# Eight offsets modulo 256 bytes for the weights' high and low parts

## The chip, the cores and the metric

The kernel runs on one core of one Trainium2 chip. The metric is device time in microseconds (us) of one execution of the whole program. Two timed runs of the kernel before gave 2563.72 and 2564.82 us, median 2564.27 us.

## The reference

Two layers on one sequence of 256 positions by 2048 channels, all in float32. Layer 0 is a multi-scale retention of 8 heads, layer 1 a causal attention of 16 heads with a relative-position bias (with 256 positions there is one block, so its block selection never picks anything else). After each comes a gated feed-forward net with a causal convolution of width 3. Nearly all the work is in the products with weights:

```
proj = h @ w_in                 # 2048 x 12288   (q, k, v, g of layer 0)
y @ w_out                       # 4096 x 2048
q, k, v = h @ w_qkv             # 2048 x 6144    (layer 1)
o @ w_out                       # 2048 x 2048
u = h @ w_up ;  ... @ w_down    # 2048 x 11264 and 5632 x 2048, in both layers
```

Each of the two mixers and each feed-forward net starts from an RMS norm and adds its output to the residual; a last RMS norm ends it.

## The kernel before, in words

**Products in high and low parts.** TensorE is fed `float32r` operands. To keep float32 accuracy, each operand is kept as two: a high part (the value copied to `float32r`) and a low part (the value less its high part). A product is then three: high by high, high by low, low by high. Activations are split once and kept (`hT`, `yT`, `actT`, `oT`: for each 128 channels 256 columns of high parts and 256 of low ones). Weights are split as they stream in.

**The stream of weights.** All weights pass through one list of units, each 1 MB: 128 partitions by 2048 floats. SP loads a unit into a tile `raw` (line 153, pool `wraw`, four buffers). Each unit is worked off in halves of 1024 floats (or four parts, where seven products take the place of eight). For each half `issue_split` (line 184) takes a tile `wh` and a tile `wl` of 128 x 1024 `float32r`, 4096 bytes a partition, from the pools `whi` and `wlo` (lines 104, 105, 191, 192), four buffers each. ScalarE (ACT) copies `raw` to `wh` (line 222), VectorE (DVE) subtracts `wh` from `raw` into `wl` (line 223). Line 238 and lines 243, 244 form sums of weight blocks inside `raw` for the seven-product form. `parts[i]` then hands views of both tiles to the matmuls of half `i`.

**The order.** `step` (line 252) issues the splits up to three halves ahead (`LOOKAHEAD`), then the matmuls of one half. A tile `wh` or `wl` comes free when the last matmul that reads it has run; with four buffers, the split of half `i` waits for half `i-4`. In the program built from this, the four buffers of each pool are used in a fixed rotation, but for two places (the 17th and 18th and the 633rd and 634th tile), where two neighbours come in the other order.

**Three kinds of panel use them.**

- `panel_b` (line 330) produces transposed results: a 128 x 128 block of `wh` or `wl` is the stationary operand, which a weight load brings into TensorE, and `xT[k]` of `hT` streams past it: 512 columns (high and low) for `wh` (line 345), 256 columns (high) for `wl` (line 348). One step over `c` is two loads and matmuls of each kind. The q and k projections and both up projections go this way.
- `panel_s` (line 358) and `panel_a` (line 304): a 128 x 128 block of the activations is stationary, and 512 columns of `wh` or `wl` stream past it (line 391, and lines 311 to 313). The v and g projections, the output projections and the down projections go this way; lines 523 to 525 (`mm3`) do the small products of retention and attention, line 541 and 1152 transposes against an identity (`ident`, inside the tile `laid`).

**Where the tiles lie.** The pools are laid one behind the other in each partition, each tile rounded up to 32 bytes. In the program before, `hT` starts at byte 18112, the four `raw` tiles at 56256 and every 8192 bytes on, `wh` at 89024, 93120, 97216 and 101312, `wl` at 105408, 109504, 113600 and 117696, and behind `sml` and `scr` the tiles `yT`, `actT` and `oT`. All of these leave 192 when divided by 256, and all the slices that TensorE reads of them begin at a multiple of 512 bytes in their tile. `h` starts at 0 modulo 256, `ident` at 128, `sg` and `e` at 192.

Of the kernel before, what the change touches and what calls it, by code (L numbers as in the profile page):

```python
# [11 lines left out]
F32R = mybir.dt.float32r  # L12
# [5 lines left out]
P = 128  # L18
# [80 lines left out]
def build(tc, a, out):  # L99
    nc = tc.nc  # L100
    ctx = ExitStack()
    cst = ctx.enter_context(tc.tile_pool(name="cst", bufs=1))
    wraw = ctx.enter_context(tc.tile_pool(name="wraw", bufs=4))
    whi = ctx.enter_context(tc.tile_pool(name="whi", bufs=4))
    wlo = ctx.enter_context(tc.tile_pool(name="wlo", bufs=4))
    sml = ctx.enter_context(tc.tile_pool(name="sml", bufs=2))
    scr = ctx.enter_context(tc.tile_pool(name="scr", bufs=1))
    pacc = ctx.enter_context(tc.tile_pool(name="pacc", bufs=2, space=bass.MemoryType.PSUM))
# [42 lines left out]
    def issue_dma(u):  # L151
        src, n = units[u]
        raws[u] = wraw.tile([P, 2048], F32, name="raw")
        dst = raws[u].rearrange("p (c n) -> p c n", n=n)
        if len(src.shape) == 4:
            for b in range(2):
                nc.sync.dma_start(dst[:, :, b * 512 : (b + 1) * 512], src[:, :, b, :])
        elif u == 2:

            load_x(8, 12)  # L160
            nc.sync.dma_start(dst[:, :4], src[:, :4])
            load_x(12, 16)
            nc.sync.dma_start(dst[:, 4:], src[:, 4:])
        else:
            nc.sync.dma_start(dst, src)
        if u in consts:
            consts[u]()

    def first_dmas():
        (src0, n), (src1, _) = units[:2]  # L170
        for u in range(2):
            raws[u] = wraw.tile([P, 2048], F32, name="raw")
        dst0, dst1 = (raws[u].rearrange("p (c n) -> p c n", n=n) for u in range(2))
        load_x(0, 2)
        nc.sync.dma_start(dst0[:, :2], src0[:, :2])
        load_x(2, 4)
        nc.sync.dma_start(dst0[:, 2:4], src0[:, 2:4])
        nc.sync.dma_start(dst1[:, :4], src1[:, :4])
        load_x(4, 8)
        nc.sync.dma_start(dst0[:, 4:], src0[:, 4:])  # L180
        nc.sync.dma_start(dst1[:, 4:], src1[:, 4:])
        state["dma"] = 2

    def issue_split(i):
        u, split_part = order[i]
        if i == 0:
            first_dmas()
        while state["dma"] <= min(u + (1 if i < 8 else 2), len(units) - 1):
            issue_dma(state["dma"])
            state["dma"] += 1  # L190
        wh = whi.tile([P, 1024], F32R, name="wh")
        wl = wlo.tile([P, 1024], F32R, name="wl")
        if i == 0:
            r = raws[u]

            def split(sl):
                split_to(wh[:, sl], wl[:, sl], r[:, sl])

            def rest():
                x_T(2, 2)  # L200
                split(slice(512, 1024))
                for _ in range(2):
                    issue_split(state["split"])
                    state["split"] += 1

            hi, lo = x_T_parts(0, 2)
            hi(0)
            act.activation(wh[:, :S], r[:, :S], AF.Copy)
            lo(0)
            hi(1)  # L210
            dve.tensor_tensor(wl[:, :S], r[:, :S], wh[:, :S].bitcast(F32), op=ALU.subtract)
            lo(1)
            split(slice(S, 512))
            fillers(FILLERS)
            midway[0, 1] = rest
        else:
            split_part(raws[u], wh, wl)
        n = min(units[u][1], 512)
        parts[i] = (wh.rearrange("p (c n) -> p c n", n=n), wl.rearrange("p (c n) -> p c n", n=n))

    def split_to(hi, lo, src):
        in_turn(act.activation(hi, src, AF.Copy))  # L222
        in_turn(dve.tensor_tensor(lo, src, hi.bitcast(F32), op=ALU.subtract))  # L223
# [28 lines left out]
    def step(n):  # L252
        i = state["mm"]
        ahead = 0 if i == 0 else 1 if i < 3 else 2 if i < 8 else LOOKAHEAD
        while state["split"] <= min(i + ahead, n - 1):
            issue_split(state["split"])
            state["split"] += 1
        halves[i]()
        state["mm"] += 1
# [302 lines left out]
    def x_T(c0, n, how=to_T):  # L562
        return how(hT, c0, lambda t, c: h[:, t, (c0 + c) * P : (c0 + c + 1) * P], c0, n)

    def x_T_parts(c0, n):
        return x_T(c0, n, to_T_parts)
# [115 lines left out]
    def fillers(n):  # L682
        for _ in range(n):
            pe.matmul(warmup[:, :P], lhsT=ones, rhs=ones, start=True, stop=True)
# [556 lines left out]
```

## Time and profile before

| what | value |
|---|---|
| timed runs | 2563.72, 2564.82 us |
| profiled execution, first to last instruction (its span) | 2563.1 us |
| instructions | 34486 |
| granted TensorE clock, mean | 0.999 |

The profiled execution has no time of its own beside the span; the timed runs lie 0.6 and 1.7 us above it.

By stage (busy us of each engine in the stretch):

| stretch, us | stage | PE | PEld | DVE | ACT |
|---|---|---|---|---|---|
| 0 to 75 | start, q and k of head 0 | 72.05 | 59.88 | 61.53 | 47.41 |
| 75 to 515 | retention heads | 439.91 | 372.93 | 386.48 | 236.53 |
| 515 to 741 | last head, output projection | 226.00 | 187.45 | 201.97 | 129.97 |
| 741 to 1234 | up projection, layer 0 | 493.00 | 429.47 | 377.84 | 277.98 |
| 1234 to 1508 | down projection, v of attention | 273.51 | 225.70 | 251.98 | 165.56 |
| 1508 to 1735 | attention | 227.00 | 199.02 | 159.51 | 118.95 |
| 1735 to 1845 | output projection | 110.00 | 91.70 | 90.96 | 64.30 |
| 1845 to 2337 | up projection, layer 1 | 492.00 | 428.89 | 377.22 | 278.40 |
| 2337 to 2563 | down projection, end | 217.55 | 179.30 | 200.58 | 128.43 |

How to read it: PE are the matmuls, PEld the weight loads, which run beside them. Both are pipelined, so the busy time of a matmul (its ns in a row) is longer than the distance from one matmul's start to the next one's; that distance, the pace, is read from start times or from a run of matmuls in the chain of waits. L345 is line 345 of the kernel.

### The profile page before, as it was taken

The numbers are of one execution on the slowest core, as the hardware profiler recorded it, in microseconds if no ns is written. First come the engines' busy times: TensorE is split into PE (matmuls) and PEld (weight loads), VectorE is DVE, ScalarE is ACT, GpSimd is POOL, SyncE is SP. The second block draws the span as 40 slices with busy tenths as digits, with TensorE's granted clock in tenths as the row PEclk, the third lists the DMA queues.
The fourth block names the chain that finished last, engine by engine and source line by source line (L and its number), as shares of the span: only waits on it lengthen the run. The fifth ranks groups of instructions, "written<-read, shape, count | busy, mean of one in ns | idle before, by whom it ended". The sixth has DMA issues, their size and how long they took to land.

```text
span 2563.1 us, 34486 instructions
## 1 busy us (share of the span) xinstructions
PE 2551.0 (100%) x13277; PEld 2174.4 (85%) x13277; DVE 2108.1 (82%) x2766; ACT 1447.5 (56%) x1870; POOL 10.2 (0%) x24
## 2 busy tenths in 40 slices
PE   9999999999999999999999999999999999999998
PEld 7888888888888888888888888888888888888887
DVE  7888888998877777777898887768877777778997
ACT  6555555555555555555565655555655555555654
POOL 0000000000000000000000000000000000000000
PEclk9999999999999999999999999999999999999999
DMA  7665555555565555556665565555556556557654
GB/s 258 229 202 181 197 192 186 182 183 195 197 197 190 197 194 197 194 197 193 234 210 194 198 214 177 175 180 175 194 190 197 194 193 198 192 198 240 215 198 148
DMA packets 342196, 504.41 MB, mean 197 GB/s; under 512 B 9600, under 2 KB 260496, under 8 KB 341776
## 3 DMA queue, kind: packets, MB, share of 16 engines
q1 hardware_dynamic: 330672, 483.53, 56.4%
q10 hardware_dynamic: 11360, 18.69, 2.2%
q8 instruction: 104, 1.70, 0.3%
q14 instruction: 60, 0.49, 0.1%
HBM read 494.82 MB, written 10.51 MB: 197 GB/s over the span
## 4 chain that ended last, share of the span: by engine, by line
PE 95%; DVE 2%; issue 1%; ACT 1%; DMA 1%; SPq 0%; POOL 0%; POOLq 0%; ACTq 0%; DVEq 0%
PE acc L345 34%; PE aux L391 32%; PE acc L348 17%; PE acc L391 8%; DVE wl L223 1%; PE acc L311 1%; PE acc L313 1%; PE acc L312 1%; PE aux L524 0%; PE aux L525 0%; PE aux L523 0%; PE aux L541 0%; DMA raw<-in_ret_w_in_dram 0%; ACT wh L222 0%; DMA f<-t 0%
## 5 line engine op out<-in xcount | busy, mean ns | idle before, releaser
L222 ACT ACTIVATE wh<-raw 128x1024 fp32r<-128x1024 f32 (+2 forms) x1067 | 1084.5, 1028 | 1012.5 <-PE acc L345 439.3
L223 DVE TENSOR_TENSOR wl<-raw,wh 128x1024 fp32r<-128x1024 f32 (+2 forms) x1067 | 1242.0, 1181 | 394.6 <-ACT wh L222 386.6
L345 PE MATMUL acc<-hT,wh 128*128 128x512 f32 x3840 | 1208.8, 396 | 1.0 <-DVE hT L547 0.8
L348 PEld LDWEIGHTS acc<-hT,wl 128*128 128x128 f32 x3840 | 721.0, 188 | 170.4 <-DVE wl L223 0.8
L348 PE MATMUL acc<-hT,wl 128*128 128x256 f32 x3840 | 755.3, 278 | 0.2 <-DVE wl L223 0.2
L345 PEld LDWEIGHTS acc<-hT,wh 128*128 128x128 f32 x3840 | 586.1, 189 | 3.4 <-ACT wh L222 1.6
L391 PE MATMUL aux<-wh,actT 128*128 128x512 f32 x976 | 319.4, 390 | 0.0
L391 PE MATMUL aux<-wh,hT 128*128 128x512 f32 x942 | 314.6, 391 | 0.3 <-ACT wh L222 0.2
L391 PEld LDWEIGHTS aux<-wh,actT 128*128 128x128 f32 x976 | 183.2, 188 | 38.4 <-DVE h L621 0.5
L391 PEld LDWEIGHTS aux<-wh,hT 128*128 128x128 f32 x942 | 176.8, 188 | 38.7 <-ACT wh L222 1.7
L391 PE MATMUL aux<-wl,actT 128*128 128x512 f32 x488 | 189.9, 389 | 0.0
L391 PE MATMUL aux<-wl,hT 128*128 128x512 f32 x471 | 183.8, 390 | 0.4 <-DVE wl L223 0.4
L930 DVE SCALAR_TENSOR_TENSOR t<-u,cw,t 128x256 f32<-128x256 f32 x352 | 146.6, 478 | 0.0
L391 PE MATMUL aux<-wh,yT 128*128 128x512 f32 x426 | 141.8, 391 | 0.4 <-ACT yT L222 0.4
L391 PE MATMUL acc<-wh,hT 128*128 128x512 f32 x358 | 131.6, 391 | 0.0
L391 PEld LDWEIGHTS aux<-wl,actT 128*128 128x128 f32 x488 | 91.6, 188 | 18.8
L391 PEld LDWEIGHTS aux<-wl,hT 128*128 128x128 f32 x471 | 88.4, 188 | 19.1 <-DVE wl L223 1.1
L926 ACT ACTIVATE t<-u,cw 128x256 f32<-128x256 f32 x176 | 94.9, 586 | 0.1
L391 PEld LDWEIGHTS aux<-wh,yT 128*128 128x128 f32 x426 | 80.0, 188 | 17.6 <-ACT yT L222 0.9
L238 DVE TENSOR_TENSOR raw<-raw 128x1024 f32<-128x1024 f32 x77 | 93.6, 1216 | 0.0
L391 PE MATMUL aux<-wl,yT 128*128 128x512 f32 x213 | 83.0, 390 | 0.0
L746 DVE TENSOR_TENSOR bs<-acc,bs 128x512 f32<-128x512 f32 x120 | 81.9, 683 | 0.0
(228 smaller groups left out, 1940.4 us busy)
## 6 DMA issues: line engine op xcount, KB each, us to landing
raw<-in_ffn_w_up_dram SPq DMA_DIRECT2D x176, 1024.0 KB, 5.1
raw<-in_ffn_w_down_dram SPq DMA_DIRECT2D x88, 1024.0 KB, 5.5
raw<-in_ret_w_in_dram SPq DMA_DIRECT2D x133, 512.0 KB, 4.5
raw<-in_moba_w_qkv_dram SPq DMA_DIRECT2D x48, 1024.0 KB, 5.3
raw<-in_ret_w_out_dram SPq DMA_DIRECT2D x32, 1024.0 KB, 5.4
raw<-in_ret_w_in_dram SPq DMA_DIRECT2D x29, 1024.0 KB, 5.5
raw<-in_moba_w_out_dram SPq DMA_DIRECT2D x16, 1024.0 KB, 5.3
f<-t ACTq DMA_DIRECT2D x20, 256.0 KB, 4.2
```

The lines of the kernel that those rows point to most:

```text
L222: in_turn(act.activation(hi, src, AF.Copy))
L223: in_turn(dve.tensor_tensor(lo, src, hi.bitcast(F32), op=ALU.subtract))
L238: dve.tensor_tensor(b[:, 0:2, :], b[:, 0:4:3, :], b[:, 1:2, :].to_broadcast([P, 2, 512]), op=ALU.add)
L311: pe.matmul(acc, lhsT=xh, rhs=wh[:, c, :], start=(k == 0), stop=False)
L312: pe.matmul(acc, lhsT=xh, rhs=wl[:, c, :], start=False, stop=False)
L313: pe.matmul(acc, lhsT=xl, rhs=wh[:, c, :], start=False, stop=(k == nk - 1))
L345: pe.matmul(acc[:, b, :], lhsT=wh[:, c, b * P : (b + 1) * P], rhs=xt[:, k, :], start=(k == 0), stop=False)
L348: pe.matmul(acc[:, b, S:], lhsT=wl[:, c, b * P : (b + 1) * P], rhs=xt[:, k, :S], start=False, stop=(k == KC - 1))
L391: pe.matmul(acc[b], lhsT=xs, rhs=ws, start=(n == 1), stop=(n == uses[b]))
L746: dve.tensor_tensor(bs, acc[:, :, :S], bs, op=ALU.add)
L926: act.activation(t[:, i, :], u[:, i, 2:], AF.Identity, bias=c[:, 3, b : b + 1], scale=c[:, 2, b : b + 1])
L930: dve.scalar_tensor_tensor(t[:, i, :], u[:, i, tap : tap + S], c[:, tap, b : b + 1], t[:, i, :], op0=ALU.mult, op1=ALU.add)
```

## The change

The two pools get one buffer for each of eight tags (`wh0` to `wh3`, `wl0` to `wl3`) in place of four buffers under one name. A tile is 1032 floats long, 4128 bytes, in place of 4096, and half `i` takes the tag `i % 4`. Of the 1032 floats it uses 1024, from the first one on, or for `wh2` and `wl3` from the fifth on (16 bytes further). Nothing else is edited.

```
-    whi = ctx.enter_context(tc.tile_pool(name="whi", bufs=4))
-    wlo = ctx.enter_context(tc.tile_pool(name="wlo", bufs=4))
+    whi = ctx.enter_context(tc.tile_pool(name="whi", bufs=1))
+    wlo = ctx.enter_context(tc.tile_pool(name="wlo", bufs=1))
...
+    def part_tile(pool, name, i, starts):
+        n = i % 4
+        return pool.tile([P, 1032], F32R, name=name, tag=f"{name}{n}")[:, starts[n] : starts[n] + 1024]
+
     def issue_split(i):
...
-        wh = whi.tile([P, 1024], F32R, name="wh")
-        wl = wlo.tile([P, 1024], F32R, name="wl")
+        wh = part_tile(whi, "wh", i, (0, 0, 4, 0))
+        wl = part_tile(wlo, "wl", i, (0, 0, 0, 4))
```

4128 is 16 x 256 + 32, so each tile in the row starts 32 bytes further round the 256 than the one before. With the tiles laid in the order in which they are first taken, the parts used begin at 192, 224, 16 and 32 modulo 256 (`wh0` to `wh3`) and at 64, 96, 128 and 176 (`wl0` to `wl3`). Five of the eight (224, 16, 32, 96, 176) are no multiple of 64; all are multiples of 16. The eight tiles together are 256 bytes longer, so all that lies behind them moves by 256 bytes and keeps its offset modulo 256.

## Prediction

> **What bounds the kernel now.** I read the page first, then the chain of waits, then PE's own waits, then a stretch of the timeline.
>
> ```profile
> span 2563.1 us, 34486 instructions
> ...
> PE 2551.0 (100%) x13277; PEld 2174.4 (85%) x13277; DVE 2108.1 (82%) x2766; ACT 1447.5 (56%) x1870; POOL 10.2 (0%) x24
> ...
> PE 95%; DVE 2%; issue 1%; ACT 1%; DMA 1%; SPq 0%; POOL 0%; POOLq 0%; ACTq 0%; DVEq 0%
> ```
>
> PE is busy all through and holds 95% of the chain that ends last. So the time is the number of matmuls by their pace, and a change of addresses can matter in two ways only: it changes PE's pace, or it makes PE wait. PE's waits for the split tiles are (weight loads, the longest of them; engine, line, what was waited for: us in total, times, longest):
>
> ```profile
> PEld aux L391 <- ACT wh L222: 1.7, 4, 0.6
> PEld acc L345 <- ACT wh L222: 1.6, 2, 1.0
> ...
> PEld aux L391 <- DVE wl L223: 1.1, 2, 0.8
> ...
> PEld acc L391 <- DVE wl L223: 0.9, 1, 0.9
> PEld acc L348 <- DVE wl L223: 0.8, 2, 0.6
> ```
>
> Together 6.1 us in 2563: the splits arrive in time. What is left is the pace. For panel_s it stands in the chain of waits (start us, us, what):
>
> ```profile
> 74.65 5.44 PE aux L391 x24
> ...
> 123.51 5.44 PE aux L391 x24
> ...
> 604.27 5.44 PE aux L391 x24
> ...
> 1254.84 5.44 PE aux L391 x24
> ```
>
> 24 matmuls of 512 columns take 5.44 us, 226.7 ns each, in layer 0's first head, in the output projection and in the down projection alike, with hT, yT or actT as the stationary operand. For panel_b I take the timeline (start us, us, engine and line; L345 x2 opens each step over c):
>
> ```profile
> 999.74 0.62 PE L345 MATMUL acc<-hT,wh 128*128 128x512 f32 x2
> ...
> 1000.44 0.63 PE L345 MATMUL acc<-hT,wh 128*128 128x512 f32 x2
> 1000.46 1.06 ACT L222 ACTIVATE wh<-raw 128x1024 fp32r<-128x1024 f32 x1 [1.74 <-PE acc L345]
> ...
> 1001.13 0.63 PE L345 MATMUL acc<-hT,wh 128*128 128x512 f32 x2
> ...
> 1001.43 0.58 ACT L745 ACTIVATE bs<-acc 128x512 f32<-128x512 f32 x1
> 1001.56 1.23 DVE L223 TENSOR_TENSOR wl<-raw,wh 128x1024 fp32r<-128x1024 f32 x1 [1.57 <-ACT wh L222]
> ...
> 1001.83 0.63 PE L345 MATMUL acc<-hT,wh 128*128 128x512 f32 x2
> ...
> 1002.53 0.63 PE L345 MATMUL acc<-hT,wh 128*128 128x512 f32 x2
> ...
> 1010.89 0.63 PE L345 MATMUL acc<-hT,wh 128*128 128x512 f32 x2
> ```
>
> From 999.74 to 1010.89 are 16 steps: 696.9 ns each, for two matmuls of 512 and two of 256 columns. The reader should see what does not change the step. From 999.74 to 1000.44 DVE is idle from 999.99 on and ACT throughout: 0.70. From 1000.44 to 1001.13 ACT writes a wh tile and DVE is idle: 0.69. From 1001.83 to 1002.53 DVE reads raw and wh and writes wl, with ACT at work too at first: 0.70. If these engines' accesses met PE's in the memory, at one offset modulo 256 or at any, steps with them would be longer. They aren't. Accesses of ACT and DVE cost PE nothing that these 10 ns show.
>
> **The change part by part.** It adds and removes no instruction: the same 1067 splits, 13277 matmuls and loads and DMAs. What can move is the duration of those that touch wh or wl, and the order in which the tiles come free.
>
> ```profile
> L345 PE MATMUL acc<-hT,wh 128*128 128x512 f32 x3840 | 1208.8, 396 | 1.0 <-DVE hT L547 0.8
> L223 DVE TENSOR_TENSOR wl<-raw,wh 128x1024 fp32r<-128x1024 f32 x988 | 1193.2, 1222 | 394.6 <-ACT wh L222 386.6
> L222 ACT ACTIVATE wh<-raw 128x1024 fp32r<-128x1024 f32 x988 | 1035.6, 1059 | 980.2 <-PE acc L345 439.3 <-PE aux L391 193.4 <-issue 155.2
> L348 PE MATMUL acc<-hT,wl 128*128 128x256 f32 x3840 | 755.3, 278 | 0.2 <-DVE wl L223 0.2
> ...
> L391 PE MATMUL aux<-wh,actT 128*128 128x512 f32 x976 | 319.4, 390 | 0.0
> ...
> L746 DVE TENSOR_TENSOR bs<-acc,bs 128x512 f32<-128x512 f32 x120 | 81.9, 683 | 0.0
> ...
> L921 DVE TENSOR_TENSOR u<-bs,rBs 128x512 f32<-128x512 f32 x88 | 60.9, 692 | 3.1
> ...
> L223 DVE TENSOR_TENSOR wl<-raw,wh 128x512 fp32r<-128x512 f32 x78 | 53.2, 683 | 0.0
> ...
> L621 DVE TENSOR_TENSOR h<-h,rBs 128x512 f32<-128x512 f32 x16 | 10.9, 683 | 0.1
> ```
>
> *DVE and ACT.* L223 on 512 columns has both inputs at 192 modulo 256 and takes 683 ns; L621 has h at 0 and rBs at 192 and takes 683 too. Inputs at one offset or at two: no difference, so I take 0. The other bound is L921, which writes u eight bytes past a 32-byte boundary (and reads one input repeated): 692 against 683 of L746, 1.3%. On all of L223 that is 1.3% of 1246 us, 16 us of DVE, in either direction. It is covered by DVE's idle time. The tightest stage is that of the retention heads; first all engines, then L223 alone (stretch: length, busy us):
>
> ```profile
> 75.00:515.00 440.00, 439.91 (x2211) 372.93 (x2210) 386.48 (x505) 236.53 (x285) 5.06 (x8) 1.00 0.59 195
> ```
>
> ```profile
> 75.00:515.00 440.00, 218.99 (x192) 1.00 0.59 195
> ```
>
> DVE has 440.00 - 386.48 = 53.5 us free there, so L223's 219.0 us could grow by 24% before DVE fills the stage. Without that cover the price would be the 16 us, 2580. ACT at 56% has more room. Term: 0.
>
> *PE's pace.* Each matmul reads wh or wl, as the stream (panel_s) or through its weight load (panel_b); its other operand stays at 192. The trace has no PE operand at 16 or 32 modulo 64, but it has one pair of the same work at two offsets, the transposes of L541, where the streamed identity is at 128 and the stationary operand is h at 0 or sg at 192 (ns min/median/max):
>
> ```profile
> L541 PEld LDWEIGHTS acc<-laid,h x64: 138/139/145, 717.5 to 1829.0; 128*128 128x128 f32 x64
> L541 PE MATMUL acc<-laid,h x64: 270/272/331, 717.7 to 1829.1; 128*128 128x128 f32 x64
> L541 PEld LDWEIGHTS aux<-laid,sg x56: 138/141/143, 95.8 to 506.4; 128*128 128x128 f32 x56
> L541 PE MATMUL aux<-laid,sg x56: 272/273/273, 95.9 to 506.5; 128*128 128x128 f32 x56
> ```
>
> 272 against 273, 139 against 141: the load and the matmul take no notice of where the stationary operand lies relative to the stream, 128 apart or 64. I take 0.
>
> The bounds. For a gain, the most that a meeting of PE's own two reads could cost now is the part of the pace that isn't columns. Two equations: 512 s + f = 226.7 and 1536 s + 4 f = 696.9, s ns a column and f ns a matmul with its load. Four times the first less the second gives 512 s = 209.9, so f = 16.8 ns; times 13277 that is 223 us. The nearest row that could be such a meeting is smaller: L345's 396 ns against L391's 390 for the same 512 columns, 6 ns x 3840 = 23 us. For a loss, DVE's 1.3% put on the five tiles of eight that leave the 64-byte raster: 2551 x 5/8 x 1.3% = 21 us. f rests on one fixed cost in both panels, which the trace can't prove; a cost at each switch of weights would explain it without any address, and accesses of ACT and DVE at any phase left PE's step even, so I stay near the small bounds.
>
> The Trainium skill, "TensorE: Matmul & The Clock Gate", part 1, gives back-to-back matmuls of 512 columns 215.7 ns start to start; against the row's 226.7 that leaves 11.0 ns for what comes with each weight load, an estimated 146 us for all, and 2418 if the new offsets removed it. The same page, part 2 (step 1, LDWEIGHTS), states that stationary and streamed operand have independent read ports and that a load takes no bandwidth from the running matmul; by that the 11 ns are no conflict and the change is worth 0. The even step of the trace agrees with the second.
>
> *The order of the tiles.* Before, a split takes whichever tile comes free; after, tile i % 4. In the program before the two are the same but at the two places named above. There a split may wait for the half before it, 16 matmuls at 174 ns (696.9 / 4) = 2.8 us, and splits run three halves ahead, which hides it: 0, at most 2 x 2.8 = 5.6 us. Behind such a wait on ACT stands the next split, and behind that PE. A gain is bounded by the 6.1 us of PE's waits above.
>
> Sum: 2563.1 + 0 = 2563.1 for a profiled span; the runs shown have a median of 2564.27, 1.2 above it, and I carry that: 2564.3 us.
>
> **The rivals.**
>
> *A, faster: PE's two reads meet.* Before, stationary and streamed operand both start at 192; after, seven tiles of eight start elsewhere. For it: f is unexplained, and equal offsets are the rule everywhere in the matmuls. Against it: L541's two rows, and that ACT's and DVE's accesses, which pass PE's at every distance, cost it nothing. Price: 23 us by the nearest row, 2541; all of f would give 2341. It passes 2% (51 us) when 3.9 ns a matmul go.
>
> *B, slower: a start off the 64-byte raster costs PE a piece more.* Place: the five tiles at 224, 16, 32, 96 and 176, in 13277 x 5/8 = 8298 matmuls. For it: L921 shows a small price of an odd start on DVE, and no PE row shows such a start to be free. Against it: only the start of an operand of 512 or 2048 bytes would pay. Price: 21 us by DVE's 1.3%, 2585; with the 6 ns between L345 and L391 on each of the 8298, 50 us, 2614. It decides for slower by over 2% from 6.2 ns on. By the Trainium skill, "SBUF — State Buffer", section on the DMA port swizzle, SBUF is read in lines of 16 bytes; all eight starts are multiples of 16, so by that rule B costs nothing. No row here shows it.
>
> *C: the fixed tags make splits wait*, up to 5.6 us, 2570. PE's short waits speak against it.
>
> *D: the tiles don't move*, if each were rounded up to 256 bytes. Tiles of 8 bytes lie 32 apart before, so no. It would give 2564.3 as well and counts with the forecast.
>
> **How the numbers follow.** Forecast (with D) 0.79, its own range 2558 to 2570 (6 us of waits either way); A 0.11, of which 0.07 over 2%; B 0.07, of which 0.04 over 2%; C 0.03. 2% is about what a measurement of this kernel can tell from no change. So faster 0.07, slower 0.04, the same 0.89. The range goes to the small bounds of A and B, 2541 to 2585; left out are about 0.09 of A and 0.05 of B.
>
> **What would show it.** Right: 24 matmuls of L391 still 5.44 us, a step of panel_b still 696.9 ns, L345 at 396 and L348 at 278, L223 within 1.3% of 1222. A would show as a step under 690 ns or L391 under 225 ns; B as L391's 24 longer than 5.50 us, for some tiles and not for others; C as PEld waits for wh or wl beyond 6 us. The prediction is wrong if PE's pace moves by 2 ns a matmul or more (27 us).

## The result: 28.5 us slower, in the pace of the matmuls

The changed kernel takes 2592.78 us (median of 2592.6 and 2592.97) against 2564.27, a ratio of 1.011 with an interval of 1.0081 to 1.0139. The forecast was 2564.3 and the range ended at 2585.

The page of the profile after, its span, busy times and chain by engine:

```profile
span 2590.8 us, 34479 instructions
...
PE 2579.6 (100%) x13277; PEld 2181.4 (84%) x13277; DVE 2110.7 (81%) x2766; ACT 1450.2 (56%) x1870; POOL 10.2 (0%) x24
...
PE 98%; DVE 1%; issue 0%; DMA 0%; ACT 0%; SPq 0%; POOLq 0%; POOL 0%; ACTq 0%
```

As many matmuls and loads as before, and PE holds still more of the chain. So it isn't waiting longer. The weight loads' waits for the splits, after (the edit moves the lines by four: L391 is now L395, L345 is L349, L348 is L352, L222 is L226, L223 is L227):

```profile
PEld acc L349 <- ACT wh L226: 1.6, 2, 1.0
PEld aux L395 <- DVE wl L227: 1.5, 5, 0.7
PEld aux L395 <- ACT wh L226: 1.3, 5, 0.3
```

4.4 us, where it was 6.1. The groups by shape show that the splits run as they did, and where the time went:

```profile
L349 PE MATMUL acc<-hT,wh 128*128 128x512 f32 x3840 | 1204.4, 395 | 1.4 <-DVE hT L551 1.2 <-ACT wh L226 0.2
L227 DVE TENSOR_TENSOR wl<-raw,wh 128x1024 fp32r<-128x1024 f32 x988 | 1194.3, 1222 | 420.6 <-ACT wh L226 418.9
L226 ACT ACTIVATE wh<-raw 128x1024 fp32r<-128x1024 f32 x988 | 1037.4, 1060 | 1002.9 <-PE acc L349 438.2 <-PE aux L395 228.0 <-issue 161.6
L352 PE MATMUL acc<-hT,wl 128*128 128x256 f32 x3840 | 764.3, 280 | 0.0
...
L395 PE MATMUL aux<-wh,actT 128*128 128x512 f32 x976 | 324.2, 394 | 0.0
```

DVE's subtraction takes 1222 ns as before and ACT's copy 1060 for 1059. The matmul of L395 went from 390 to 394, that of L352 from 278 to 280. These are modelled ends; the pace is read from starts. From the chain of waits (start us, us, what), in the retention heads and in the output projection:

```profile
124.46 5.58 PE aux L395 x24
...
193.63 5.59 PE aux L395 x24
...
602.69 5.59 PE aux L395 x24
...
634.04 5.58 PE aux L395 x24
```

24 matmuls of 512 columns took 5.44 us and now take 5.58. And 16 steps of panel_b on the timeline:

```profile
1013.04 0.62 PE L349 MATMUL acc<-hT,wh 128*128 128x512 f32 x2
...
1024.22 0.62 PE L349 MATMUL acc<-hT,wh 128*128 128x512 f32 x2
```

11.18 us, where it was 11.15.

To see this tile by tile, I matched the matmuls of the trace, in order, with those of the program, which carry the addresses. A "triple" is the three matmuls of panel_s on one stationary pair (high by high, high by low, low by high), a "step" the four matmuls of panel_b; those over 760 ns, or with something else between, are left out. Before, 1520 triples take 681.3 ns on average (680 in the median) and 1824 steps 696.9.

| half (bytes of wh, wl beyond the other operands) | triple after, ns | step after, ns |
|---|---|---|
| 0, 128 | 696.9 | 699.8 |
| 32, 160 | 696.6 | 703.5 |
| 80, 192 | 693.3 | 698.9 |
| 96, 240 | 701.7 | 693.7 |
| mean over all | 697.0 | 699.0 |

(697.0 - 681.3) / 3 = 5.2 ns a matmul, times 4953 matmuls in panel_s and panel_a, would be 25.9 us; (699.0 - 696.9) ns times 1920 steps 4.0 us. That is 29.9 where the span grew by 27.7: the means leave out what lies between panels and the waits. Added up from start to start over every matmul, panel_s and panel_a went from 1131.8 to 1155.3 us, panel_b from 1343.1 to 1347.4, all others from 78.7 to 78.6: 23.5 and 4.3 us, the whole of it. So the loss is in the pace, most of it where the weights are streamed. There every half has its part in it, between 693.3 and 701.7 ns; of the steps, those of the half at 96 and 240 became shorter, 693.7 ns.

### The profile page after: what moved, and what is told of

It is laid out like the page before. It is cut to its first block, busy times and chain, and to the rows that moved or that the text cites. A ratio compares the mean times of both kernels' runs of the same rounds, so it can differ in the third digit from the quotient of the medians.

```text
span 2590.8 us, 34479 instructions
## 1 busy us (share of the span) xinstructions
PE 2579.6 (100%) x13277; PEld 2181.4 (84%) x13277; DVE 2110.7 (81%) x2766; ACT 1450.2 (56%) x1870; POOL 10.2 (0%) x24
## 4 chain that ended last, share of the span: by engine, by line
PE 98%; DVE 1%; issue 0%; DMA 0%; ACT 0%; SPq 0%; POOLq 0%; POOL 0%; ACTq 0%
PE acc L349 34%; PE aux L395 34%; PE acc L352 17%; PE acc L395 8%; PE acc L316 1%; PE acc L315 1%; PE acc L317 1%; PE aux L545 0%; PE aux L528 0%; PE aux L529 0%; PE aux L527 0%; PE acc L545 0%; DMA raw<-in_ret_w_in_dram 0%; DVE wl L227 0%; PE aux L1156 0%
## 5 line engine op out<-in xcount | busy, mean ns | idle before, releaser
L226 ACT ACTIVATE wh<-raw 128x1024 fp32r<-128x1024 f32 (+2 forms) x1067 | 1086.8, 1028 | 1040.9 <-PE acc L349 438.2
L227 DVE TENSOR_TENSOR wl<-raw,wh 128x1024 fp32r<-128x1024 f32 (+2 forms) x1067 | 1243.4, 1182 | 420.6 <-ACT wh L226 418.9
L349 PE MATMUL acc<-hT,wh 128*128 128x512 f32 x3840 | 1204.4, 395 | 1.4 <-DVE hT L551 1.2
L352 PEld LDWEIGHTS acc<-hT,wl 128*128 128x128 f32 x3840 | 720.7, 188 | 166.8
L352 PE MATMUL acc<-hT,wl 128*128 128x256 f32 x3840 | 764.3, 280 | 0.0
L349 PEld LDWEIGHTS acc<-hT,wh 128*128 128x128 f32 x3840 | 589.3, 188 | 4.0 <-ACT wh L226 1.6
L395 PE MATMUL aux<-wh,actT 128*128 128x512 f32 x976 | 324.2, 394 | 0.0
L395 PE MATMUL aux<-wh,hT 128*128 128x512 f32 x942 | 318.3, 395 | 0.0
L395 PEld LDWEIGHTS aux<-wh,actT 128*128 128x128 f32 x976 | 183.1, 188 | 43.8
L395 PEld LDWEIGHTS aux<-wh,hT 128*128 128x128 f32 x942 | 176.7, 188 | 43.0 <-ACT wh L226 1.3
L395 PE MATMUL aux<-wl,actT 128*128 128x512 f32 x488 | 192.2, 394 | 0.0
L395 PE MATMUL aux<-wl,hT 128*128 128x512 f32 x471 | 185.5, 395 | 0.3 <-DVE wl L227 0.3
L395 PE MATMUL aux<-wh,yT 128*128 128x512 f32 x426 | 143.9, 395 | 0.3 <-ACT yT L226 0.3
L395 PE MATMUL acc<-wh,hT 128*128 128x512 f32 x358 | 133.1, 395 | 0.0
L395 PEld LDWEIGHTS aux<-wl,actT 128*128 128x128 f32 x488 | 91.7, 188 | 21.3
L395 PEld LDWEIGHTS aux<-wl,hT 128*128 128x128 f32 x471 | 88.5, 188 | 21.6 <-DVE wl L227 1.5
L395 PEld LDWEIGHTS aux<-wh,yT 128*128 128x128 f32 x426 | 79.9, 188 | 19.8 <-ACT yT L226 0.7
L395 PE MATMUL aux<-wl,yT 128*128 128x512 f32 x213 | 84.0, 395 | 0.0
```

The costliest lines, as they stand in the source:

```text
L349: pe.matmul(acc[:, b, :], lhsT=wh[:, c, b * P : (b + 1) * P], rhs=xt[:, k, :], start=(k == 0), stop=False)
L352: pe.matmul(acc[:, b, S:], lhsT=wl[:, c, b * P : (b + 1) * P], rhs=xt[:, k, :S], start=False, stop=(k == KC - 1))
L395: pe.matmul(acc[b], lhsT=xs, rhs=ws, start=(n == 1), stop=(n == uses[b]))
```

## The experiments

In each kernel the edit moves the line numbers by a few; the tiles' names tell the groups apart. Five theories. DISTANCE: what counts is how far the streamed operand starts from the stationary one, modulo 256, whichever tiles they are. RASTER: a start off a multiple of 64 costs, wherever the other operand lies (rival B of the prediction). ALTERNATION: PE pays when the next streamed operand starts elsewhere than the last. ORDER: the fixed tags make splits wait (rival C). ENGINES: what counts is how wh and wl lie to raw, in the reads and writes of ACT and DVE.

### e1_tags: the tags without the offsets

```
-        wh = whi.tile([P, 1024], F32R, name="wh")
-        wl = wlo.tile([P, 1024], F32R, name="wl")
+        wh = whi.tile([P, 1024], F32R, name="wh", tag=f"wh{i % 4}")
+        wl = wlo.tile([P, 1024], F32R, name="wl", tag=f"wl{i % 4}")
```

(and `bufs=1` in both pools.)

> Only the fixed tags of the change, tiles 4096 bytes long, all eight back at 192 modulo 256. Theory ORDER (the fixed rotation makes splits wait): about 2592 us. Every theory in which the offsets do it: 2564 us within 3, 24 matmuls of a streamed panel in 5.44 us, 16 steps of panel_b in 11.15 us.

Measured: 2564.27 us, ratio 0.9997 (0.9987 to 1.0006). The chain of waits:

```profile
123.79 5.44 PE aux L391 x24
...
133.99 5.44 PE aux L391 x24
```

ORDER falls: all of the loss comes with the offsets.

### e4_all_32: every operand moved together

```
-    sums = cst.tile([P, 48], F32, name="sums")
+    sums = cst.tile([P, 56], F32, name="sums")
```

> All operands from hT on, wh, wl and the activations, moved by 32 bytes together to 224 modulo 256: equal among themselves, but off the raster of 64. DISTANCE and ALTERNATION: 2564 us within 3, triples of 680 ns. RASTER: 2590 us or more, triples of 695 or more.

Measured: 2564.7 us, ratio 0.9999 (0.9989 to 1.0008); triples 681.3, steps 696.9 ns. The chain:

```profile
133.70 5.44 PE aux L391 x24
...
143.90 5.44 PE aux L391 x24
```

RASTER falls: all that PE reads of hT, wh, wl and the activations behind them now starts at 224 modulo 256, off a multiple of 64, and nothing is lost. At this one step of 32 no absolute place matters.

### e2_pairs_a and e3_pairs_b: wh and wl of a half at one offset

One pool in place of two, the tiles in the order wh0, wl0, wh1, wl1 and so on, with lengths and starts that put each pair at its place; for e2:

```
+    def part_tile(name, i, sizes):
+        length, start = sizes[i % 4]
+        return wsp.tile([P, length], F32R, name=name, tag=f"{name}{i % 4}")[:, start : start + 1024]
...
+        wh = part_tile("wh", i, ((1032, 8), (1024, 0), (1024, 0), (1024, 0)))
+        wl = part_tile("wl", i, ((1032, 0), (1032, 0), (1032, 0), (1056, 0)))
```

> wh and wl of one half share an offset; the four halves lie 32, 64, 96 and 128 bytes beyond the other operands (hT, yT, actT, oT, which stay at 192 modulo 256). A triple of the streamed panels (high by high, high by low, low by high) took 680 ns before and 692 to 702 after the change. Theory DISTANCE (what counts is how far the streamed operand starts from the stationary one, modulo 256): every half off 680, 690 to 702, time 2580 to 2600 us. Theory RASTER (a start off a multiple of 64 costs): the halves at 64 and 128 beyond stay at 680, those at 32 and 96 at 695 or more, time about 2578. Theory ALTERNATION (cost when the next streamed operand starts elsewhere than the last): all at 680, 2564 to 2567 us.

> As e2_pairs_a with the four halves 0, 160, 192 and 224 bytes beyond. DISTANCE: the half at 0 has 680 ns a triple, the others 690 to 702, time 2578 to 2595 us. RASTER: 0 and 192 at 680, 160 and 224 at 695 or more, about 2578. ALTERNATION: all at 680, 2564 to 2567 us.

Measured: e2 2600.41 us, ratio 1.0138 (1.0121 to 1.0155); e3 2590.97, ratio 1.0101 (1.0086 to 1.0116). By half:

| bytes beyond the other operands | triple, ns | step, ns |
|---|---|---|
| e2: 32 | 699.8 | 701.7 |
| e2: 64 | 690.3 | 697.3 |
| e2: 96 | 704.2 | 705.8 |
| e2: 128 | 700.3 | 703.4 |
| e3: 0 | 688.6 | 699.6 |
| e3: 160 | 700.7 | 707.6 |
| e3: 192 | 699.4 | 691.9 |
| e3: 224 | 697.8 | 695.4 |

ALTERNATION falls: within a half, wh and wl start at one offset, and no half is at 680. RASTER falls again: it gave 680 ns to the halves at 64, 128 and 192, and they have 690.3, 700.3 and 699.4. DISTANCE passes, but not clean: e2's time and its half at 96 lie just past their ranges (2600 us, 702 ns), and it gave the half at 0 680 ns, and that has 688.6. The trace shows more of this last one. In e3, wl's matmuls on the timeline (one in three), first in a half at 0, then, from 604.81 on, in one at 160:

```profile
602.06 0.40 PE L394 MATMUL aux<-wl,yT 128*128 128x512 f32 x1
...
602.76 0.39 PE L394 MATMUL aux<-wl,yT 128*128 128x512 f32 x1
...
603.45 0.39 PE L394 MATMUL aux<-wl,yT 128*128 128x512 f32 x1
...
604.12 0.39 PE L394 MATMUL aux<-wl,yT 128*128 128x512 f32 x1
...
604.81 0.39 PE L394 MATMUL aux<-wl,yT 128*128 128x512 f32 x1
...
605.51 0.40 PE L394 MATMUL aux<-wl,yT 128*128 128x512 f32 x1
...
606.21 0.40 PE L394 MATMUL aux<-wl,yT 128*128 128x512 f32 x1
```

Within the half at 0 the distances shorten, 0.70, 0.69, 0.67; in the half at 160 they stay at 0.70. Over all halves at 0, the first triple takes 695.9 ns, the second 687.4, the third 681.7 and the fourth 680.5; at 160 it is 698.1, 703.8, 700.4 and 702.4. So a half at distance 0 finds its pace again only after the first two triples, six matmuls, when one at another distance went before. The change has no half with both tiles at 0: the first has wh at 0 and wl at 128.

### e5_raw_96: the source of the splits moved

```
-    rBs = cst.tile([P, 2 * S], F32, name="rBs")
+    rBs = cst.tile([P, 2 * S + 24], F32, name="rBs")[:, : 2 * S]
```

and a tile of 160 bytes behind raw, so that wh and all after it stay at 192 modulo 256.

> Only raw, the source of the splits, moved by 96 bytes; all that TensorE reads stays at 192 modulo 256. Theory DISTANCE (the streamed operand's start against the stationary one's): 2564 us within 3, triples of the streamed panels at 680 ns, steps of panel_b at 697. Theory ENGINES (what counts is how wh and wl lie to raw, through the reads and writes of ACT and DVE): 2580 to 2600 us, triples 690 or more.

Measured: 2564.64 us, ratio 1.0 (0.999 to 1.0009); triples 680 ns in the median, steps 696.9.

```profile
123.62 5.45 PE aux L393 x24
...
133.84 5.44 PE aux L393 x24
```

ENGINES falls at the one distance tried: each tile now starts 160 bytes beyond raw, modulo 256, as wl1 does in the change. (e6 to e9 below add the other side: there the pace changes with raw, wh and wl where they were.) This kernel also puts wh and wl 256 bytes further from hT, and the pace is the same; a move by 256 does nothing, where one by 64 or 128 does.

### e6 to e9: hT moved instead

Here the weights stay where they were. hT gets 64 floats more and begins at another float in each of its four lives (retention, first feed-forward net, attention, second feed-forward net):

```
+    hT_room = cst.tile([P, KC * 2 * S + 64], F32R, name="hT")
+    hT_starts = [4, 8, 12, 16]
+
+    def next_hT():
+        n = hT_starts.pop(0)
+        xT_h[:] = [hT_room[:, n : n + KC * 2 * S].rearrange("p (k s) -> p k s", s=2 * S)]
...
+            if i == 0:
+                after(4, next_hT)
```

> Only hT moved, within a longer tile, by another amount in each of its four lives: 16 bytes in retention, 32 in the feed-forward net of layer 0, 48 in attention, 64 in that of layer 1. wh, wl, raw, yT, actT and oT stay at 192 modulo 256. DISTANCE: panels with yT, actT or oT as stationary operand keep 226.7 ns a matmul; those with hT leave it (229 to 235 ns), and steps of panel_b differ from life to life, between 688 and 708 ns, steady within a life. ENGINES: all panels as before, 2564 us.

> As e6_hT_16_64 with 80, 96, 112 and 128 bytes. DISTANCE: panels with hT off 226.7 ns a matmul and off 697 ns a step, the others as before. ENGINES: all as before, 2564 us.

> As e6_hT_16_64 with 144, 160, 176 and 192 bytes. DISTANCE: panels with hT off 226.7 ns a matmul and off 697 ns a step (where the weights lay 192 bytes beyond hT, in e3_pairs_b, a step took about 690, so some distance in this scan may be faster for panel_b), the others as before. ENGINES: all as before, 2564 us.

> hT moved by 8 bytes in retention, 56 in the feed-forward net of layer 0, 4 in attention, 72 in that of layer 1; the transformed activations of the output and down projections stay at distance 0. DISTANCE with a smooth curve: steps of panel_b near those of the neighbours measured, 690 to 697 ns at 56 and 72 (64 took 690), 697 at 8 and 4. DISTANCE by lines of 16 bytes: 56 as 48 or 64 (702 or 690), 72 as 64 or 80 (690 or 704), 4 and 8 as 0 (697). Panels with actT, yT, oT: 680 ns a triple.

Single runs: 2564.72, 2586.6, 2575.67 and 2587.57 us, each a mixture of four distances. What counts is the pace by distance (mean ns; the feed-forward nets give 697 steps to a distance, the other lives some 210; triples are those with hT as the stationary operand, some 400 in retention, 30 to 72 in the other lives; the row at 0 is the kernel before):

| hT beyond the weights, bytes | step | triple |
|---|---|---|
| 0 | 696.9 | 681.3 |
| 4 | 717.8 | 698.0 |
| 8 | 708.0 | 693.5 |
| 16 | 696.8 | 684.0 |
| 32 | 693.4 | 695.6 |
| 48 | 702.2 | 699.7 |
| 56 | 700.0 | |
| 64 | 690.1 | 699.9 |
| 72 | 708.0 | |
| 80 | 703.6 | 696.3 |
| 96 | 706.7 | 696.0 |
| 112 | 699.5 | 699.9 |
| 128 | 696.7 | 701.9 |
| 144 | 698.9 | 688.3 |
| 160 | 703.3 | 698.8 |
| 176 | 706.1 | 690.8 |
| 192 | 693.4 | 687.3 |

The rows at 4, 48, 112 and 176 are those of attention, where a step takes 699.6 ns in the kernel before too (696.1 to 696.7 in the other lives). Against that, 112 costs nothing.

On the timeline this is 16 steps in the first feed-forward net, of e6 (32 bytes) and then of e7 (96 bytes):

```profile
989.66 0.62 PE L353 MATMUL acc<-hT,wh 128*128 128x512 f32 x2
...
1000.75 0.62 PE L353 MATMUL acc<-hT,wh 128*128 128x512 f32 x2
```

```profile
989.98 0.63 PE L353 MATMUL acc<-hT,wh 128*128 128x512 f32 x2
...
1001.29 0.63 PE L353 MATMUL acc<-hT,wh 128*128 128x512 f32 x2
```

11.09 and 11.31 us, for the same matmuls on weights that lie as they did before. Triples whose stationary operand is yT or actT stay at a median of 680 in e6, e8 and e9 (689.5 for yT in e7, where they take turns with triples on sums of activation blocks, which are kept in hT). The two scans can also be laid side by side: weights x bytes beyond hT are hT 256 - x bytes beyond the weights.

| weights beyond (e2, e3) | step | triple | hT beyond (e6 to e8) | step | triple |
|---|---|---|---|---|---|
| 64 | 697.3 | 690.3 | 192 | 693.4 | 687.3 |
| 96 | 705.8 | 704.2 | 160 | 703.3 | 698.8 |
| 128 | 703.4 | 700.3 | 128 | 696.7 | 701.9 |
| 160 | 707.6 | 700.7 | 96 | 706.7 | 696.0 |
| 192 | 691.9 | 699.4 | 64 | 690.1 | 699.9 |
| 224 | 695.4 | 697.8 | 32 | 693.4 | 695.6 |

The steps come in the same order both times, but for one tie; the triples differ by up to 5.4 ns, and the same distance has the shortest. So the pace follows the distance between the two operands of PE, whichever of them is moved: DISTANCE stands. Not all that was expected under its name came: at 16 and 128 bytes the steps (696.8 and 696.7) did not leave 697, and at 16 and 144 most triples stayed at 680. Of the expectations for e9, both finer forms fail: 8 bytes took 708.0 and 4 took 717.8, neither as 0 nor between 0 and 16, and 72 took 708.0, neither as 64 nor as 80.

The chain of e6 shows that a distance can have two paces. Retention at 16 bytes:

```profile
123.77 5.60 PE aux L399 x24
...
134.16 5.44 PE aux L399 x24
...
144.36 5.44 PE aux L399 x24
```

5.60 at 124, close to the change's 5.58, and 5.44 from 134 on. Triple by triple, hT at 16 bytes runs at 680 ns up to 47 us, at some 700 from 51 to 129, and at 680 from 131 on. At 144 bytes (e8), too, two thirds of the triples take 680 and most of the others some 700. So the triple means of these two rows are of two paces, not of one.

### e11_no_16: the change without the two starts 16 bytes in

```
-        wh = part_tile(whi, "wh", i, (0, 0, 4, 0))
-        wl = part_tile(wlo, "wl", i, (0, 0, 0, 4))
+        wh = part_tile(whi, "wh", i, (0, 0, 0, 0))
+        wl = part_tile(wlo, "wl", i, (0, 0, 0, 0))
```

> The change without its two starts 16 bytes into the tile: wh at 0, 32, 64, 96 and wl at 128, 160, 192, 224 beyond the other operands. If the loss of the change came from those two odd starts (theory LINE16): 2564 to 2570 us. DISTANCE: six of the eight distances are as they were and the other two are off 0 as well: 2580 to 2600 us, triples of the half at wh 0, wl 128 at about 697 ns as in the change.

Measured: 2590.29 us, ratio 1.01 (1.0084 to 1.0115), the change's loss but for 2.5 us. The half at 0 and 128, the same in both kernels, has triples of 690.9 here, where 697 was expected as in the change (696.9). That the other halves reach into it would fit e3; no run shows it by itself. LINE16 falls.

### e10_hT_64: a version faster than both

The table has a distance at which panel_b is faster than at 0, and in the feed-forward nets hT is read by panel_b alone. The edit is that of e6 with starts 0, 16, 0 and 16 floats, and the transformed activations that the down projections keep in hT stay at the old place:

```
+    hT_starts = [0, 16, 0, 16]
...
+    hT = hT_room[:, : KC * 2 * S].rearrange("p (k s) -> p k s", s=2 * S)
```

> hT moved by 64 bytes in the two feed-forward nets, where no streamed panel reads it, and at its old place else. DISTANCE, with the 690.1 ns a step that 64 bytes took in e6_hT_16_64 against 697.0: 1408 steps x 6.9 ns = 9.7 us less, about 2555 us, ratio 0.996; triples at 680. Were the step of 690 an accident of that run and not of the distance: 2564 us.

Measured: 2555.41 us, ratio 0.9964 (0.9952 to 0.9977). 1394 steps at 64 take 690.1 ns, 432 at 0 697.9, triples 680 in the median. 16 steps of the first feed-forward net, and the chain:

```profile
1000.02 0.62 PE L354 MATMUL acc<-hT,wh 128*128 128x512 f32 x2
...
1011.06 0.62 PE L354 MATMUL acc<-hT,wh 128*128 128x512 f32 x2
```

```profile
123.61 5.44 PE aux L400 x24
...
133.81 5.44 PE aux L400 x24
```

11.04 us, and 5.44 where nothing was moved. The table, made from other runs, gave 2555 beforehand: the distance sets the time.

## Why the prediction was wrong

**Splits, DVE, ACT, order: right.** L227 stayed at 1222 ns, PE's waits for the splits went from 6.1 to 4.4 us, and the fixed tags alone cost nothing (e1). These terms, taken as 0, were 0.

**The step that failed is "PE's pace ... I take 0".** It measured 23.5 us in the streamed panels and 4.3 in panel_b, 2.1 ns a matmul over all 13277. What sets it is the distance between PE's own two operands. Two readings led to the 0.

- *L541's two rows.* They compare a stationary operand 128 bytes from the stream with one 64 from it, and find 272 against 273 ns. But the question was equal against unequal, and both are unequal. In the panels with hT the triples at 64 and 128 bytes took 699.9 and 701.9, as alike as L541's rows, and both some 20 ns over those at 0. The control was blind to what the change does; the trace before held no matmul in these panels at any distance but 0. The rows are also lengths of single instructions and not the pace. By start times the transposes follow one another every 109 ns (median) at 128 bytes, at 64 and, in e4, at 96; no run has them at 0, so whether they heed the distance at all stays open.
- *ACT's and DVE's accesses cost PE nothing*, read from even steps. That was true (e5). It says nothing of PE's own two reads, and the prediction let it stand for them.

**The rule weighed there.** The Trainium skill, "TensorE: Matmul & The Clock Gate", part 2 (step 1, LDWEIGHTS), states that a load takes no bandwidth from the running matmul, through a port of its own. The forecast followed it, and called the even step of the trace an agreement, though that step had both operands at one offset. Here three matmuls of a triple move by up to 23 ns (704.2 against 681.3) and four of a step by 18 (717.8 against 699.6, both in attention) with nothing changed but how the operands lie; the measurement decides. Whether it is the load's read that meets the stream's wasn't shown; no run here has the one without the other.

**Rival A had the place and the wrong sign.** It was PE's two operands, but the equal offsets that I took for a possible conflict had, for the streamed panels, the shortest mean of all the distances measured. **Rival B had the sign and a size that holds** (21 to 50 us; 28.5 measured) **and the wrong mechanism**: e4 puts every start off 64 and loses nothing, and in the change the half at 0 and 128, whose tiles begin at 192 and 64, on B's raster, is as slow as the others (696.9 ns). That its size fits is luck. B's lower price, borrowed from DVE, set the range's end at 2585; its upper one, the 6 ns between L345 and L391, would have held. That price was taken for a rival and not for the bound of an operation that the trace didn't show. Rival C falls with e1, rival D with the tiles' addresses, which move as the change says.

**What stays open**: which access is delayed, why a distance can have two paces, and whether the longer steps at 4, 8 and 72 bytes belong to the distance or to the start itself, since e9 moved hT alone. By the Trainium skill, "SBUF — State Buffer", section on the DMA port swizzle, lines are 16 bytes long; the rows off a multiple of 16 (717.8, 708.0, 700.0 and 708.0 ns at 4, 8, 56 and 72 bytes) are the only ones here that bear on it, and they don't separate the two.

## What to carry to other kernels

When a trace holds an operand at one relation only, a control at two other relations tells nothing about leaving it: bound that term by the largest difference between like rows, not by the kindest. Where TensorE is busy all through, a change in how its two operands lie to each other can cost or gain a few ns a matmul. In a kernel like this one, keep the stationary and the streamed operand at one offset modulo 256 bytes unless a measured distance is better, and give all buffers of a rotation the same one. Read pace from the starts of a run of matmuls: 5.44 against 5.58 us for 24 is plain there, while the page shows PE at 100% both times.

## What the runs showed of the hardware that was not expected

The pace of load and matmul depends on the distance of the two operands modulo 256: 680 to 704 ns for three of 512 columns, 690 to 708 for two of 512 and two of 256 at multiples of 16, up to 718 at 4 bytes. The best of the distances measured isn't the same for both panels: 0 for the streamed weights, 64 for hT streaming past the weights. Pace has a memory: after another distance, PE takes some six matmuls to come back to 226.7 ns (e3), and at 16 bytes the same kernel ran at 5.60 and later at 5.44 us for 24 (e6).
